# A hybrid decoder step on one core: another memory order of the weight slots, gating by the recurrence's groups, the first slice projected whole, token tiles padded to 128

## The chip, the cores and the metric

The kernel runs on one core of one Trainium2 chip, as one program that is launched once. The metric is the time of that core in microseconds (us) of the device; lower is better. A kernel's time is the median of several runs, and one further run is recorded by the hardware profiler. The engines are named as in the profile: PE is TensorE's matrix multiplication, PEld its loading of weights, DVE is VectorE, ACT is ScalarE, POOL is GpSimd and SP is SyncE, which here only issues DMAs.

## What is computed

The reference is one inference step of a two-layer decoder. 1104 rows of 1024 features go through it: 64 rows of eight decode requests, 16 learned rows and a prompt of 1024 tokens. Layer 0 is an mLSTM mixer, a recurrence over chunks of tokens; layer 1 is an attention with forget gates over one shared K and V. A SwiGLU feed-forward network (FFN) of width 2816 follows each. Cut to the part that the change touches, the mixer of layer 0 is:

```python
p = xn @ w_in                       # q, k, v, output gate og, gates gi and gf
li = softcap(gi + b_ig)
lf = log_sigmoid(softcap(gf + b_fg))
h, state = mlstm_sequence(q, k, v, li, lf, (C0, n0, m0), lead)
h = rmsnorm(h, mh_g)                # per head
out = (h.reshape(B, T, HV) * sigmoid(og)) @ w_out
```

After it come `x = x + out` and the FFN `x + (silu(xn @ w_gate) * (xn @ w_up)) @ w_down`, and then layer 1 in the same manner.

## The kernel before, in words

**Precision by three products.** Every large product is made of three matmuls (`mm3`, lines 270 to 273): operands are split into a rounded high half and a remainder, and high·high, high·low and low·high are added up. ACT makes the high half of a piece of weights (a cast, L333), DVE the low half (a subtraction, L334). A piece of 128 columns of a 1024-row weight is 512 KB.

**Tiling.** Rows are divided in two ways. The recurrence goes by nine chunks `TTA`, the first of 80 rows and eight of 128; its groups of three, `GRP`, span the ranges `TSA`: (0, 336), (336, 720), (720, 1104), at most `SLA` = 384 wide. Everything from the output projection on goes by three equal slices `TS` of `SL` = 368 rows, and where rows must lie on partitions, by tiles `TT` of 128, 128 and 112 rows in each slice. The split activations of slice t are in two tiles of `KT * SLA` columns (`flat_x`, made by `new_x`), of which a view `X[t]` shows only the rows that count.

**Gates of the recurrence.** `cache_prep` (L932) prepares the decode cache's forget values in a pool `cp` that is closed again, and stores them with eight DMAs on POOL's queue (L960). `rec_prep` (L965) then allocates the gate bias `gbias` and the initial `m0` in the pool `rp` and loads them over POOL's queue (L971 to L974). L1015 adds the bias to the gates, L1016 to L1019 and `log_sigmoid` turn them into `li` and `lf`, and TensorE transposes both (L1031).

**Recurrence.** In `recurrence` the orders of PE, DVE, ACT and POOL are fixed by the order in which the program names the instructions. Into the steps of the chunks a generator `rest_out` puts matmuls of the remaining q, k and og projections (`f(n)`: n steps of eight). When a group of chunks is done, `norm_heads` makes the factors of the per-head norm and scales the chunk's values (L1450). `gate_head` then takes one head of a group: TensorE transposes the values of its chunks (L1478), DVE multiplies them with the norm's gain and with the sigmoid of the output gate, which is loaded from DRAM (`ogD`) into a tile `og` or `ogc` (L1479), and `split` writes high and low halves into `X`. Two groupings exist for this: `GRPA`, chunks (0, 1, 2, 3), (4, 5, 6), (7, 8), for the norm, and `GG`, overlapping groups of chunks with row ranges that end at the ends of the slices, for the gating. From chunk 6 on, `g` calls `gate(0)` and then `gate(1)` in place of `f` once the projections are used up; what is left of group 1, and all of group 2, is gated in `mlp`.

**Output projection.** `mlp` (L479) allocates ten slots on the right side of the memory, 0 to 9 in that order; slots 0 and 1 are raw buffers for weights, 2 to 5 and 6 to 9 high and low halves. Layer 1 and its attention later take the same block: `both` (slots 0 and 1 in one), 7, 3, 8, 2. Pieces of `w_out` are loaded by SP (L537), m = 0, 3, 6 into a buffer of their own and the others into slots 0 and 1, and split. After the split of m = 1 the scaling of the last group's values (`late`) is put in DVE's order. `unit(t, m, x)` projects 128 output columns m of slice t (`fm_cols`, 24 matmuls), adds the result to the residual `H[t]`, and updates the sum of squares for the norm. PE's order is fixed there. With the mLSTM layer in front (`heads` given), three units of slice 0 stand first with the remaining heads of group 1 between them, and then units of slices 0 and 1 in turn, one head of group 2 after each; `mix.zero`, the work on slice 0 with which the FFN begins, starts after unit (0, 7). Layer 1 uses the `else` branch: slice 0 whole, then slice 1 with `mix.zero` between its units.

**Token tiles.** `tm_proj` and `first_values` use tiles of tokens as TensorE's stationary operand: `x_tile` returns columns a to b of `X[t]`, so that it is 128, 128 and 112 wide in a slice. `norm_x` fills `X` with the normed rows.

**Attention.** `last_gate` (in `attend_prompt`) and the projections before it read weights split into pairs of slots: the last one, m = 6, uses slots 3 and 8. `load_k` (L2551) loads the first pair of heads' q and k into the slots 2, 7, 3, 8 of layer 1 over SP's queue; `scores` (L2635) multiplies them.

Of the kernel before, what the change touches and what calls it, by code (L numbers as in the profile page):

```python
# [7 lines left out]
F32 = mybir.dt.float32  # L8
# [8 lines left out]
P = 128  # L17
# [17 lines left out]
GRPA = [(0, 1, 2, 3), (4, 5, 6), (7, 8)]  # L35
GG = [((0, 1, 2, 3), 0, TTA[3][1]), ((4, 5, 6), TTA[3][1], TS[1][1]), ((6, 7, 8), TS[2][0], T)]
# [218 lines left out]
class Net:  # L255
# [155 lines left out]
    def norm_x(self, H, t, g, sp, pp, inplace=False, psum=False):  # L411
# [68 lines left out]
    def mlp(self, H, w, l, heads=None, cb=None, early=None):  # L480
# [8 lines left out]
        with self.pool(self.uid("nsp")) as sp, self.pool(self.uid("npp"), bufs=2, space=PSUM) as pn:  # L489
# [16 lines left out]
            if cb:  # L506
                cw = cb
                wp = cw.enter_context(self.pool(self.uid("slots"), side="right"))
                slots = {x: wp.tile([P, self.wmin if x in (0, 1, 2, 3, *LOW[:2]) else KT * P], F32 if x < 2 else F32R,
                                    name=self.uid("slot")) for x in range(10)}  # L510
            else:
                cw, slots, ws = early
                wp = cw.enter_context(self.pool(self.uid("slots"), side="right"))
                for x in (4, 9, 5, 6):
                    slots[x] = wp.tile([P, KT * P], F32R, name=self.uid("slot"))
            with ExitStack() as c:
# [3 lines left out]
                if heads:  # L520
                    gp.tile([P, 4 * SL], F32, name="rest")
# [44 lines left out]
                if heads:  # L566
                    gate, *_ = heads(c.enter_context(self.pool("ghp", bufs=2, space=PSUM)), "gh",
                                     lambda n: gp.tile([P, SL], F32, name=n, tag="og", bufs=3), 1)
                    for x in range(3):
                        unit(0, x, x)  # L570
                        for _ in range(2):
                            gate(1)
                    while gate(1):
                        pass
                    load(nc.gpsimd, 1)
                    H2 = [2]
                    for t, m in ((0, 3), (1, 0), (1, 1), (0, 4), (1, 2), (0, 5), (1, 3), (0, 6), (1, 4), (0, 7), (1, 5),
                                 (1, 6), (1, 7)):
# [11 lines left out]
                else:  # L590
                    for m in range(KT):
                        unit(0, m, m)
                    run = mix.zero()
                    weights.load(0)
                    for m in range(KT):
                        unit(1, m, m)
                        next(run, None)
                        if m > 4:
                            next(run, None)
                    for _ in run:  # L600
                        pass
# [173 lines left out]
def phase_a(self, vt):  # L775
# [7 lines left out]
    with ExitStack() as c3:  # L783
# [105 lines left out]
        self.normed = set()  # L889

        def heads(pp, tag, op, deep):
# [3 lines left out]
            def ahead():  # L895
                while todo and len(ready) < 1 + deep:
                    t, h = todo.pop(0)
                    og = op(self.uid("ogc"))
                    _, a, b = GG[t]
# [10 lines left out]
            def gate(t):  # L910
                if not left[t] or t not in self.normed:
                    return False
# [17 lines left out]
        self.recurrence(kp, self.rec, v, qkD, rest, lambda gp: heads(pp, "mmA", lambda n: gp.tile([P, GG[0][2]], F32, name=n, tag="og", bufs=4), 2))  # L930
# [33 lines left out]
def rec_prep(self, kp, gates, rp, pp):  # L964
# [3 lines left out]
    if True:  # L968

        bias = rp.tile([P, 16], F32, name="gbias")  # L970
        nc.gpsimd.dma_start(bias[:, :8], I["b_ig_a"][0].partition_broadcast(P))  # L971
        nc.gpsimd.dma_start(bias[:, 8:], I["b_fg_a"][0].partition_broadcast(P))
        m0 = rp.tile([HA, NB], F32, name="m0")
# [111 lines left out]
def recurrence(self, kp, rec, v, qkD, fill, gate):  # L1085
# [18 lines left out]
    with ExitStack() as cr, self.pool("recAp", bufs=2, space=PSUM) as pp, \  # L1104
# [24 lines left out]
        with self.pool("rec2") as sets[2], self.pool("rec1", bufs=2) as rp, self.pool("rec3") as sets[0], \  # L1129
# [9 lines left out]
            for i in range(1, NT):  # L1139
# [21 lines left out]
                last = [g for g, z in enumerate(GRPA) if z[-1] == i]  # L1161
# [5 lines left out]
                if last:  # L1167
                    norm = self.norm_heads(last[0], v, rp)
# [5 lines left out]
                R, N = N, N2  # L1174
            rest()
# [252 lines left out]
def norm_heads(self, t, v, rp):  # L1428
# [3 lines left out]
    c = GRPA[t]  # L1432
    n = len(c)
    g = slice(c[0], c[-1] + 1)
    rd = rp.tile([P, len(GRPA[0]), HA], F32, name=f"rd{t}", tag="rd", bufs=1)[:, :n]
    f = self.fA[:, :n] if t == 2 else rp.tile([P, len(GRPA[0]), HA], F32, name=f"fA{t}", tag="fA", bufs=1)[:, :n]
# [16 lines left out]
    parts = [lambda x=x, i=i: part(x, i) for x, i in enumerate(c)]  # L1453
    if t == 2:
        self.late = parts
        self.normed.add(t)
        yield
        return
    for p in parts:
        p()  # L1460
        if p is parts[-1]:
            self.normed.add(t)
        yield
# [3 lines left out]
def gate_head(self, t, h, v, og, pp, tag):  # L1467

    nc = self.nc
    chunks, g0, g1 = GG[t]  # L1470
    if h == 0:
        for x in ((0, 1), (), (2,))[t]:
            self.new_x(x)
    o = TTA[chunks[0]][0]
    ps = pp.tile([P, 512], F32, name=self.uid("ghps"), tag=tag)
    for i in chunks:
        t0, t1 = TTA[i]
        nc.tensor.transpose(ps[:, t0 - o : t1 - o], v(i)[: t1 - t0, h, :DV], self.ident[: t1 - t0, : t1 - t0])  # L1478
    nc.vector.scalar_tensor_tensor(out=og, in0=ps[:, g0 - o : g1 - o], scalar=self.gain[:, G_MH + h : G_MH + h + 1],  # L1479
# [464 lines left out]
def first_values(self, fp, pp, norm):  # L1944
# [4 lines left out]
    for t in range(3):  # L1949
        vs = self.ny(f"vf{t}")[:, : 3 * 256].rearrange("p (i d) -> p i d", i=3)  # L1950
        for x, i in enumerate(GRP[t]):
            m = TT[i][1] - TT[i][0]
            ps = pp.tile([P, 512], F32, name=self.uid("tmps"), tag="f", bufs=2)
            for k in range(KT):
                wh, wl = halves[k // 4]
                xh, xl = self.x_tile(i, k)
                self.mm3(ps[:m, :256], xh, xl, wh[:, k % 4, :], wl[:, k % 4, :], k == 0, k == KT - 1)
# [915 lines left out]
```

## Time and profile before

| what | value |
|---|---|
| runs (3) | 2869.46, 2876.91, 2881.54 us |
| median | 2876.91 us |
| profiled execution | 2876.0 us |
| its span | 2874.3 us |
| mean granted clock | 0.991 |
| HBM traffic | 299.78 MB read, 96.77 MB written |

The span is what the profiler saw from the first to the last instruction; the rest of the execution's time lies around it. The page of the profile gives for each engine the time in which it was busy and its share of the span. A row of the timeline has the start, the duration, the engine, the line of the kernel, the operation with its output and inputs, their shapes and the number of such instructions in a row; a bracket behind it says how long the engine had been idle before and what released it. A row of the waits says which engine waited at which line for which work of which engine: the total in us, how many times, and the longest. A row of windows gives the busy time of PE, PEld, DVE, ACT and POOL in a stretch of the span, then the granted clock of TensorE (1 is full speed), the share of DMA time and GB/s.

### The profile page before, as it was taken

To read this page: it belongs to the slowest core of one execution; us is meant where nothing else is said; L and a number is where in the kernel's file an instruction comes from. 1 tells how busy PE (TensorE), PEld (TensorE's weight loads), DVE (VectorE), ACT (ScalarE), POOL (GpSimd) and SP (SyncE) were. 2 spreads that over 40 slices of the span, in tenths; PEclk is the share of its full clock that TensorE was granted. 3 is DMA by queue.
4 is the path that set the end of the run, shared out by engine and by line. 5 is a ranking of instruction groups with operands and counts; after the bars stand their busy time and mean duration, and the time that the engine had idled before them with its cause. 6 is when DMAs were issued, how large, how long until landed. Compare 5 with 4: busy or idle time off the path is not lost. (4 is left out here: it accounts for less than half of the span.)

```text
span 2874.3 us, 54148 instructions
## 1 busy us (share of the span) xinstructions
PE 2786.1 (97%) x20638; PEld 2662.6 (93%) x20638; DVE 1742.2 (61%) x3598; ACT 1317.1 (46%) x2629; POOL 1074.1 (37%) x1578
## 2 busy tenths in 40 slices
PE   8898998999999999999999998999999999999999
PEld 7887988999999999999999887777899999999998
DVE  6034564787877755553365542677468778775553
ACT  6122464444444434443344553777444444443432
POOL 3022333156666411117563201455316566641110
PEclk9999999999999999999999999999999999999999
DMA  6136655222222275544453685443412222237653
GB/s 216 38 101 164 172 166 158 76 75 84 84 78 78 81 276 202 194 151 149 135 168 115 221 302 184 166 146 119 152 52 83 80 84 83 79 98 246 211 194 107
DMA packets 314070, 400.08 MB, mean 139 GB/s; under 512 B 28998, under 2 KB 235826, under 8 KB 312786
## 3 DMA queue, kind: packets, MB, share of 16 engines
q1 hardware_dynamic: 277282, 277.66, 30.4%
q0 software_dynamic: 35776, 118.40, 12.4%
q8 instruction: 162, 2.65, 0.4%
q14 instruction: 98, 0.80, 0.1%
q10 hardware_dynamic: 752, 0.57, 0.1%
HBM read 299.78 MB, written 96.77 MB: 138 GB/s over the span
## 5 line engine op out<-in xcount | busy, mean ns | idle before, releaser
L334 DVE TENSOR_TENSOR slot<-slot,slot 128x1024 fp32r<-128x1024 f32 (+3 forms) x263 | 250.7, 955 | 115.9 <-ACT slot L333 111.5
L333 ACT CAST slot<-slot 128x1024 fp32r<-128x1024 f32 (+3 forms) x263 | 206.5, 787 | 229.1 <-PE dps L272 98.6
L1541 PE MATMUL m<-x0h,slot 128*128 128x368 f32 x640 | 178.5, 330 | 0.0
L1541 PE MATMUL m<-x1h,slot 128*128 128x368 f32 x640 | 174.0, 331 | 2.7 <-DVE ns L1518 0.9
L1647 POOL DMA_DIRECT2D hr<-hT x60 | 32.5, 542 | 280.2 <-DVE T_2l L334 68.5
L1541 PE MATMUL m<-x2h,slot 128*128 128x368 f32 x480 | 132.5, 330 | 0.0
L113 POOL TENSOR_TENSOR slot<-vA 128x256 f32<-128x256 f32 x80 | 75.6, 955 | 151.9 <-DMA vA<-in_w_gate_up 78.0
L113 POOL TENSOR_TENSOR slot<-Ht 128x256 f32<-128x256 f32 x80 | 75.1, 949 | 150.8 <-DMA Ht<-in_w_gate_up 79.2
L334 DVE TENSOR_TENSOR slot<-Ht,slot 128x256 fp32r<-128x256 f32 (+3 forms) x101 | 88.7, 880 | 55.7 <-ACT slot L333 55.7
L334 DVE TENSOR_TENSOR slot<-vA,slot 128x256 fp32r<-128x256 f32 (+3 forms) x101 | 88.4, 877 | 55.8 <-ACT slot L333 55.8
L409 POOL TENSOR_TENSOR ns<-ns,nq 128x368 f32<-128x368 f32 x50 | 54.1, 1083 | 178.8 <-ACT nq L407 178.1
L1541 PEld LDWEIGHTS m<-x1h,slot 128*128 128x128 f32 x640 | 115.6, 188 | 4.6 <-DVE vA L1517 1.4
L1541 PEld LDWEIGHTS m<-x0h,slot 128*128 128x128 f32 x640 | 116.1, 188 | 0.0
L1541 PE MATMUL m<-x1l,slot 128*128 128x368 f32 x320 | 105.5, 330 | 0.0
L1541 PE MATMUL m<-x0l,slot 128*128 128x368 f32 x320 | 105.5, 330 | 0.0
L2667 ACT ACTIVATE s<-s,nb 128x272 f32<-128x272 f32 (+7 forms) x126 | 98.8, 786 | 0.6 <-POOL nb L2658 0.6
L2702 ACT COPY th<-tp 128x768 f32<-128x768 f32 (+1 forms) x80 | 73.5, 920 | 47.7 <-PE tp L2694 27.4
L1541 PE MATMUL m<-T_2h,slot 128*128 128x368 f32 x320 | 94.0, 334 | 0.0
L1541 PE MATMUL m<-T_4h,slot 128*128 128x368 f32 x320 | 93.5, 333 | 0.0
L328 DVE SCALAR_TENSOR_TENSOR slot<-slot,gain,slot 128x256 fp32r<-128x256 f32 (+2 forms) x152 | 63.8, 468 | 44.6 <-ACT slot L327 42.2
L334 DVE TENSOR_TENSOR slot<-wr,slot 128x1024 fp32r<-128x1024 f32 x42 | 53.5, 1274 | 59.1 <-ACT slot L333 59.1
L1541 PEld LDWEIGHTS m<-x2h,slot 128*128 128x128 f32 x480 | 86.9, 188 | 0.0
(861 smaller groups left out, 10360.7 us busy)
## 6 DMA issues: line engine op xcount, KB each, us to landing
slot<-in_w_down SPq DMA_DIRECT2D x88, 512.0 KB, 4.3
hr<-hT POOLq DMA_DIRECT2D x60, 368.0 KB, 5.6
wr<-in_w_down SPq DMA_DIRECT2D x42, 512.0 KB, 4.1
wraw<-in_w_in_a SPq DMA_DIRECT2D x40, 512.0 KB, 4.2
vA<-in_w_gate_up SPq DMA_DIRECT2D x40, 512.0 KB, 4.0
Ht<-in_w_gate_up SPq DMA_DIRECT2D x40, 512.0 KB, 4.0
kp<-in_cache_k SPq DMA_DIRECT2D x32, 512.0 KB, 6.9
vp<-in_cache_v SPq DMA_DIRECT2D x32, 512.0 KB, 9.6
```

Of the source, the lines that this page charges most:

```text
L113: self.net.nc.gpsimd.tensor_tensor(out=o, in0=a, in1=b, op=op)
L328: nc.vector.scalar_tensor_tensor(out=lo[:, k], in0=raw[:, k], scalar=gk, in1=hi[:, k].bitcast(F32), op0=ALU.mult, op1=ALU.subtract)
L333: self.nc.scalar.copy(hi, src)
L334: self.nc.vector.tensor_tensor(out=lo, in0=src, in1=hi.bitcast(F32), op=ALU.subtract)
L409: (nc.vector if x >= late else nc.gpsimd).tensor_tensor(out=s, in0=s, in1=sq, op=ALU.add)
L1541: nc.tensor.matmul(u.b[b][:, :SL], w[p][:, k], x[q][:, k], start=new and k == i == 0, stop=k == 1 and i == 2, skip_group_check=True)
L1647: nc.gpsimd.dma_start(hraw[j], hT[t][:, 2 * c : 2 * c + 2])
L2667: nc.scalar.activation(ss[z, u], ss[z, u], AF.Exp, bias=nb[:, z : z + 1], accum_out=sm[:, u, z : z + 1])
L2702: nc.scalar.copy(th.rearrange("p x z (u h q) -> p h (x z u) q", h=2, q=64)[:, :, :n], pt[:, :, :n])
```

## The change

Five things change.

1. `gbias` and `m0` are allocated in `kp` and no longer in `rp`.
2. The ten slots are allocated in the order 3, 8, 0, 1, 2, 7, 5, 6, 4, 9.
3. `GRPA` and `GG` go. The norm of heads and the gating both go by `GRP` and `TSA`: after the chunks 2, 5 and 8, three chunks each. A head's rows of a group now belong to one slice or two, and `part` splits them into the slices they belong to. One more `gate(1)` stands after the last chunk, so that groups 0 and 1 are gated within the recurrence, and the tiles `og` are `SLA` wide.
4. In `mlp` slice 0 is projected whole, with 0, 1, 2, 1, 2, 1, 1, 0 heads of group 2 after its eight units; slice 1 follows, with `mix.zero` between its units, in both layers.
5. `x_tile` returns 128 columns of `flat_x`, except where `tm_proj` is asked for a single tile (`only`); `norm_x` clears the columns behind the slice's 368 with a memset on POOL for each of the two halves, so that the third tile's other 16 columns are zero.

```diff
-GRPA = [(0, 1, 2, 3), (4, 5, 6), (7, 8)]
-GG = [((0, 1, 2, 3), 0, TTA[3][1]), ((4, 5, 6), TTA[3][1], TS[1][1]), ((6, 7, 8), TS[2][0], T)]
...
-    def x_tile(self, i, k):
+    def x_tile(self, i, k, m=P):
...
-        t = i // 3
-        o = ts[t][0]
-        a, b = tt[i][0] - o, tt[i][1] - o
-        xh, xl = self.X[t]
-        return xh[:, k, a:b], xl[:, k, a:b]
+        a = k * SLA + tt[i][0] - ts[i // 3][0]
+        return [x[:, a : a + m] for x in self.flat_x[i // 3]]
...
             m = t1 - t0
+            w = m if only is not None else P
...
-                xh, xl = self.x_tile(i, k)
-                self.mm3(ps[:m, :n], xh, xl, wh[:, k % 4, :], wl[:, k % 4, :], k == 0, k == KT - 1)
+                xh, xl = self.x_tile(i, k, w)
+                self.mm3(ps[:w, :n], xh, xl, wh[:, k % 4, :], wl[:, k % 4, :], k == 0, k == KT - 1)
...
         xh, xl = self.new_x(t)
+        for x in self.flat_x[t]:
+            nc.gpsimd.memset(x.rearrange("p (k n) -> p k n", k=KT)[:, :, n:].bitcast(F32), 0.0)
...
-                                    name=self.uid("slot")) for x in range(10)}
+                                    name=self.uid("slot")) for x in (3, 8, 0, 1, 2, 7, 5, 6, 4, 9)}
...
                 if heads:
                     gate, *_ = heads(c.enter_context(self.pool("ghp", bufs=2, space=PSUM)), "gh",
-                                     lambda n: gp.tile([P, SL], F32, name=n, tag="og", bufs=3), 1)
-                    for x in range(3):
-                        unit(0, x, x)
-                        for _ in range(2):
-                            gate(1)
-                    while gate(1):
-                        pass
+                                     lambda n: gp.tile([P, SLA], F32, name=n, tag="og", bufs=3), 1)
                     load(nc.gpsimd, 1)
-                    H2 = [2]
-                    for t, m in ((0, 3), (1, 0), (1, 1), (0, 4), (1, 2), (0, 5), (1, 3), (0, 6), (1, 4), (0, 7), (1, 5),
-                                 (1, 6), (1, 7)):
-                        unit(t, m, m)
-                        if not gate(2) and H2:
-                            load(nc.gpsimd, H2.pop())
-                        if (t, m) == (0, 7):
-                            run = mix.zero()
-                            weights.load(0)
-                        elif t and m > 4:
-                            for _ in range(3):
-                                next(run, None)
...
+                for m in range(KT):
+                    unit(0, m, m)
+                    for _ in range((0, 1, 2, 1, 2, 1, 1, 0)[m] if heads else 0):
+                        gate(2)
+                    if heads and m == KT - 2:
+                        load(nc.gpsimd, 2)
+                run = mix.zero()
+                weights.load(0)
+                for m in range(KT):
+                    unit(1, m, m)
+                    next(run, None)
+                    if m > 4:
                         next(run, None)
-                    for _ in run:
-                        pass
+                for _ in run:
+                    pass
...
-        bias = rp.tile([P, 16], F32, name="gbias")
+        bias = kp.tile([P, 16], F32, name="gbias")
...
-        m0 = rp.tile([HA, NB], F32, name="m0")
+        m0 = kp.tile([HA, NB], F32, name="m0")
...
-                if last:
-                    norm = self.norm_heads(last[0], v, rp)
+                if i % 3 == 2:
+                    norm = self.norm_heads(i // 3, v, rp)
...
                 R, N = N, N2
+            gate(1)
             rest()
...
-    chunks, g0, g1 = GG[t]
+    g0, g1 = TSA[t]
...
-    for i in chunks:
+    for i in GRP[t]:
         t0, t1 = TTA[i]
-        nc.tensor.transpose(ps[:, t0 - o : t1 - o], v(i)[: t1 - t0, h, :DV], self.ident[: t1 - t0, : t1 - t0])
+        nc.tensor.transpose(ps[:, t0 - g0 : t1 - g0], v(i)[: t1 - t0, h, :DV], self.ident[: t1 - t0, : t1 - t0])
```

More of the change, by code (lines that the diff above doesn't have):

```diff
@@ L520, in mlp @@
                 if heads:
-                    gp.tile([P, 4 * SL], F32, name="rest")
+                    gp.tile([P, 4 * SL - 128], F32, name="rest")
                 wp = c.enter_context(self.pool(self.uid("wo")))
@@ L567, in mlp @@
                     gate, *_ = heads(c.enter_context(self.pool("ghp", bufs=2, space=PSUM)), "gh",
-                                     lambda n: gp.tile([P, SL], F32, name=n, tag="og", bufs=3), 1)
-                    for x in range(3):
-                        unit(0, x, x)
-                        for _ in range(2):
-                            gate(1)
-                    while gate(1):
-                        pass
-                    load(nc.gpsimd, 1)
-                    H2 = [2]
-                    for t, m in ((0, 3), (1, 0), (1, 1), (0, 4), (1, 2), (0, 5), (1, 3), (0, 6), (1, 4), (0, 7), (1, 5),
-                                 (1, 6), (1, 7)):
-                        unit(t, m, m)
-                        if not gate(2) and H2:
-                            load(nc.gpsimd, H2.pop())
-                        if (t, m) == (0, 7):
-                            run = mix.zero()
-                            weights.load(0)
-                        elif t and m > 4:
-                            for _ in range(3):
-                                next(run, None)
-                    for _ in run:
-                        pass
[L590 to L596, printed above, removed]
+                                     lambda n: gp.tile([P, SLA], F32, name=n, tag="og", bufs=3), 1)
+                    load(nc.gpsimd, 1)
+                for m in range(KT):
[10 more added lines that the diff above has]
+                    if m > 4:
                         next(run, None)
[L598 to L601, printed above, removed]
+                for _ in run:
+                    pass
                 run = mix.one()
@@ L888, in phase_a @@
         left = {t: list(range(HA)) for t in range(3)}
-        self.normed = set()
         def heads(pp, tag, op, deep):
@@ L910, in gate @@
             def gate(t):
-                if not left[t] or t not in self.normed:
+                if not left[t]:
                     return False
@@ L929, in phase_a @@
         next(rest)
-        self.recurrence(kp, self.rec, v, qkD, rest, lambda gp: heads(pp, "mmA", lambda n: gp.tile([P, GG[0][2]], F32, name=n, tag="og", bufs=4), 2))
+        self.recurrence(kp, self.rec, v, qkD, rest, lambda gp: heads(pp, "mmA", lambda n: gp.tile([P, SLA], F32, name=n, tag="og", bufs=4), 2))
     return heads
@@ L1160, in recurrence @@
                 squares = self.chunk_out(i, R, rp, *args, den, ssq, g, exp=N2 and N2["exp"])
-                last = [g for g, z in enumerate(GRPA) if z[-1] == i]
-                if last:
+                if i % 3 == 2:
                     for _ in squares:
@@ L1166, in recurrence @@
                 next(norm, None)
-                if last:
-                    norm = self.norm_heads(last[0], v, rp)
+                if i % 3 == 2:
+                    norm = self.norm_heads(i // 3, v, rp)
                 if i == 5:
@@ L1431, in norm_heads @@
     tm, den, ssq = self.fin
[L1432 to L1436, printed above, removed]
+    g = slice(3 * t, 3 * t + 3)
+    rd = rp.tile([P, 3, HA], F32, name=f"rd{t}", tag="rd", bufs=1)
+    f = self.fA if t == 2 else rp.tile([P, 3, HA], F32, name=f"fA{t}", tag="fA", bufs=1)
     nc.vector.scalar_tensor_tensor(out=rd, in0=den[:, g], scalar=-1.0, in1=den[:, g], op0=ALU.mult, op1=ALU.max)
@@ L1452, in part @@
             op=ALU.mult)
-    parts = [lambda x=x, i=i: part(x, i) for x, i in enumerate(c)]
+    parts = [lambda x=x, i=i: part(x, i) for x, i in enumerate(GRP[t])]
     if t == 2:
         self.late = parts
-        self.normed.add(t)
         yield
@@ L1460, in norm_heads @@
         p()
-        if p is parts[-1]:
-            self.normed.add(t)
         yield
@@ L1469, in gate_head @@
     nc = self.nc
-    chunks, g0, g1 = GG[t]
+    g0, g1 = TSA[t]
     if h == 0:
-        for x in ((0, 1), (), (2,))[t]:
-            self.new_x(x)
-    o = TTA[chunks[0]][0]
+        self.new_x(t)
     ps = pp.tile([P, 512], F32, name=self.uid("ghps"), tag=tag)
-    for i in chunks:
+    for i in GRP[t]:
         t0, t1 = TTA[i]
-        nc.tensor.transpose(ps[:, t0 - o : t1 - o], v(i)[: t1 - t0, h, :DV], self.ident[: t1 - t0, : t1 - t0])
-    nc.vector.scalar_tensor_tensor(out=og, in0=ps[:, g0 - o : g1 - o], scalar=self.gain[:, G_MH + h : G_MH + h + 1],
+        nc.tensor.transpose(ps[:, t0 - g0 : t1 - g0], v(i)[: t1 - t0, h, :DV], self.ident[: t1 - t0, : t1 - t0])
+    nc.vector.scalar_tensor_tensor(out=og, in0=ps[:, : g1 - g0], scalar=self.gain[:, G_MH + h : G_MH + h + 1],
                                    in1=og, op0=ALU.mult, op1=ALU.mult)
```

4 lines of the change are left out of this document (2 added, 2 removed).

## The prediction

> **What bounds the kernel now.** I read the page first: one engine is busy almost all the time.
>
> ```profile
> span 2874.3 us, 54148 instructions
> PE 2786.1 (97%) x20638; PEld 2662.6 (93%) x20638; DVE 1742.2 (61%) x3598; ACT 1317.1 (46%) x2629; POOL 1074.1 (37%) x1578
> ```
>
> TensorE is the bound, and 2874.3 − 2786.1 = 88.2 us of the span is all that waits can give back; beyond that only matmuls that run faster count. So the question for every part of the change is which TensorE gap it touches. The gaps were then looked up by place: the gate bias (136 to 149 us), the end of the recurrence and the start of the output projection (420 to 478), the FFN's start (553 to 640), the start of the prompt's attention (1782 to 1791). The profiled execution took 2876.0 us against a median of 2876.91 in three runs; I sum against 2876.0 and add 0.9. A measurement of this kernel can tell about 0.5% (14 us) from no change.
>
> **Gate bias and m0 in `kp` instead of `rp`.**
>
> ```profile
> 135.58 0.60 PE L954 MATMUL csps<-ident,lp 128*128 128x128 f32 x4
> 149.26 2.04 PE L1031 MATMUL rps<-ident,gates 80*8 80x80 f32 x9 [13.09 <-DVE gates L1017]
> 148.26 0.31 DVE L1015 TENSOR_TENSOR gates<-gates,gbias 128x144 f32<-128x144 f32 x1 [6.68 <-DMA gbias<-in_b_fg_a]
> 139.34 4.25 POOL L960 DMA_DIRECT2D csE<-cs  x8 [1.46 <-DVE clast L958]
> 144.12 0.55 POOL L972 DMA_DIRECT2D gbias<-in_b_fg_a  x1
> 4.74 0.22 POOL L991 MEMSET cap<- 128x128 f32 x1
> ```
>
> Columns: start, duration, engine, line, operation, and in brackets the idle time before it with its releaser. The bias is loaded into memory that cache_prep had used, so its DMAs are issued behind the eight stores of csE, at 144, and land at 148; the gate addition waits for that, and TensorE idles 13.09 us. `cap`, allocated from `kp` in the same function, is filled at 4.74 us: nothing had used its memory. In `kp` the bias can be loaded as early. Then what is late next? DVE is free after its cumulative sum:
>
> ```profile
> 139.40 0.98 DVE L1035 MEMSET rs<- 8x1104 f32 x1 [0.17 <-issue]
> 159.36 0.78 PE L1031 MATMUL rps<-ident,lf_tm 80*8 80x80 f32 x6
> 155.57 0.23 DVE L352 SCALAR_TENSOR_TENSOR lf_tm<-lf_tm,lsw 128x72 f32<-128x72 f32 x1
> ```
>
> The addition can stand where rs is cleared now, at 139.2 or before, and TensorE's nine transposes of the input gates have their operand before TensorE asks. The log-sigmoid behind it takes 155.80 − 148.26 = 7.5 us from addition to end; 139.2 + 7.5 = 146.7. TensorE transposes that result at 159.36 in before; without the gap it asks for it at 159.36 − 13.09 = 146.3. So 0.4 us of new wait, and 1.4 if the 0.98 us memset goes first. Taken: −12.7; ends −11.7 and −13.1.
>
> **The recurrence's tail.** Gating by the recurrence's own groups removes the wait of gate transposes for the scaled values, 2.4 us, but scales a group of three chunks at a time, close to the end, where each chunk costs half of the second row:
>
> ```profile
> PE ghps L1478 <- DVE vA L1450: 2.4, 2, 1.7
> 456.26 2.35 DVE L1450 TENSOR_TENSOR vA<-vA,fA 128x1024 f32<-128x1024 f32 x2
> ```
>
> The extra `gate(1)` and the changed counts move about one such 1.18 us scaling ahead of work that TensorE waits for. Transposes per head go from 4+3+3 to 3+3+3, splits from 2+1+1 to 1+2+2: one small instruction each way. Taken −1.0; ends −2.4 and +1.2.
>
> **The junction into the output projection.** Order of the slots decides where w_out's raw pieces m = 1 and 2 land. In before slots 0 and 1 lie first, over the buffers of the recurrence's gates; their load is issued only at 441.60. In after, slots 3 and 8 lie there and slots 0 and 1 over the old weight buffers, which are last read by the split of 429.13.
>
> ```profile
> PE pops L271 <- ACT wo L333: 5.5, 2, 4.0
> PE pops L273 <- DVE wo L334: 1.3, 2, 0.7
> 441.60 0.99 SPq L537 DMA_DIRECT2D slot<-in_w_out_a  x2
> 429.13 1.22 DVE L319 TENSOR_TENSOR wlo<-wraw,whi 128x1024 fp32r<-128x1024 f32 x1
> DMA to landing us min/median/max: 4.3/4.7/9.5
> 445.31 1.23 DVE L334 TENSOR_TENSOR wo<-woraw,wo 128x1024 fp32r<-128x1024 f32 x1 [1.90 <-ACT wo L333]
> 452.43 1.28 ACT L902 ACT_TABLE_LOAD   x1 [7.16 <-DMA ogc<-ogD]
> 450.00:460.00 10.00, 5.38 (x24) 4.81 (x23) 4.88 (x5) 5.18 (x7) 0.53 (x2) 0.79 0.36 101
> 460.00:470.00 10.00, 9.78 (x53) 9.36 (x52) 9.45 (x13) 6.08 (x9) 4.32 (x6) 0.87 0.97 287
> ```
>
> The first two rows are waits (total, times, longest) from 443 to 478; the two last give per stretch the busy time of PE, PEld, DVE, ACT and POOL, then the granted clock. Both longest waits, 4.0 and 0.7, belong to m = 1. It would land by 430.4 + 4.7 = 435 instead of 446 and could be cast straight behind m = 0. But one thing more held it: ACT sits 7.16 us before the table load at 452.43, waiting for a gate input, and the cast of m = 1 stands behind that sigmoid in its order. In after the first slice's units come first, with no gate after unit 0, so the cast should stand ahead of the sigmoid; then the low half of m = 1 is done by about 449.5, and TensorE asks for it near 450.4. The wait for m = 0 (1.5 + 0.6) stays. Gone: 4.0 + 0.7 = 4.7. The clock: (1 − 0.79) × 5.38 + (1 − 0.87) × 9.78 = 2.4 us of slow matmuls behind that gap. Taken −7.1; ends −3 (half of it) and −9 (with the small waits that the two rows leave out).
>
> Is the first slice's pace kept? A unit is 24 matmuls: at 53 in 9.78 us it takes 4.4 us, so eight take about 35. DVE has in it 8 low halves at 1.23, three scalings at 1.18, and for 8 accumulations, 8 gate products and 16 split pieces, 0.25 to 0.6 each, some 15: 28 us in all. It fits, with little to spare.
>
> **The FFN's start.** The loop now is layer 1's own: `mix.zero` runs between slice 1's units and not after them.
>
> ```profile
> PE m L1541 <- DVE vA L1517: 3.0, 2, 2.1
> PE m L1541 <- ACT vA L1547: 1.7, 2, 1.1
> PE m L1541 <- DVE Ht L1517: 2.2, 2, 1.4
> PE m L1541 <- DVE ns L1518: 0.9, 1, 0.9
> PE m L1541 <- ACT Ht L1547: 0.6, 1, 0.6
> 620.00:630.00 10.00, 10.00 (x53) 10.00 (x53) 7.82 (x11) 3.16 (x7) 7.54 (x8) 0.85 0.17 50
> ```
>
> The first two waits are layer 0's, the next three layer 1's, where that order runs already: 4.7 against 3.7 us. And the 10 us after layer 0's waits ran at a clock of 0.85, which costs 1.5. Taken −1.0 − 1.5 = −2.5; ends 0 and −6.2 (every wait and the clock). The Trainium skill, "TensorE: Matmul & The Clock Gate", Part 1, says that the clock falls after an idle window of about 3.4 us; the trace has 0.85 behind gaps of 2.1 us at most, so it does not follow that rule here. By the rule the 1.5 us has another cause and stays, and the sum would be 1.5 us more.
>
> **Token tiles padded to 128.** The third tile of each slice has 112 columns in TensorE's stationary operand and gets 128, in 864 matmuls. The trace has both widths side by side, 24 matmuls of 112 and then 48 of 128:
>
> ```profile
> 1299.74 0.28 PE L271 MATMUL tmps<-slot,x1h 128*112 128x256 f32 x1
> 1302.62 0.28 PE L271 MATMUL tmps<-slot,x2h 128*128 128x256 f32 x1
> 1308.27 0.28 PE L271 MATMUL tmps<-slot,x2h 128*112 128x256 f32 x1
> L273 PEld LDWEIGHTS tmps<-slot,x1l 128*112 128x112 f32 x96 | 17.1, 178 | 0.0
> L272 PEld LDWEIGHTS tmps<-slot,x1h 128*128 128x128 f32 x192 | 36.1, 188 | 0.0
> ```
>
> (1302.62 − 1299.74) / 24 = 120.0 ns a matmul at 112 and (1308.27 − 1302.62) / 48 = 117.7 at 128, although the load itself reads 178 and 188 ns. Nine groups of 96 are 864 matmuls: 864 × (117.7 − 120.0) = −2.0 us; ends 0 and −4. The 80-wide first tile of the projections ahead of the recurrence is padded too: taken as nothing, by the same rows. The six pad memsets are on POOL, 0.22 us or less each by the row of `cap`, 37% busy: nothing. If they delayed a norm it would be 1.3 us. The Trainium skill, same page, section "LDWEIGHTS (loading the stationary operand)", has the load grow with the columns, so padding should cost; the two load rows agree in sign, the pitch does not.
>
> **The attention's start.** `both` and slots 7, 3, 8, 2 of the second layer take the upper end of the same block, so the new order also changes what they lie over.
>
> ```profile
> PE sp L2635 <- DMA slot<-qDl: 4.5, 1, 4.5
> 1784.32 0.34 PE L2635 MATMUL sp<-slot,slot 64*128 64x144 f32 x2 [2.29 <-DMA slot<-kDh]
> PE sp L2635 <- DMA slot<-kDl: 1.6, 1, 1.6
> SPq L2551 <- PE bps L273: 15.3, 1, 15.3
> 1779.06 0.34 SPq L2551 DMA_DIRECT2D slot<-qDh  x1
> 1759.70 0.33 PE L271 MATMUL bps<-x0h,slot 128*128 128x368 f32 x1
> ```
>
> SyncE holds the loads of the first pair's q and k for 15.3 us, until the gate projection's last weights (pair 3 and 8) are read, at 1779. In after slots 3 and 8 lie lowest, outside the new tiles, and the last one that overlaps belongs to m = 5, whose last matmul is at 1759.70. The loads can leave 1779.06 − 15.3 = 1763.8 or a little after, and TensorE, which wants them from 1784.32 − 2.29 = 1782.0 on, finds them there: it had the first of them 5.3 us after its issue at 1779.06 and the last 12 us after, and would now have 18. Taken −4.5 − 2.3 − 1.6 = −8.4; ends −4 (the scores behind are paced by DVE, which might only move the gap) and −8.4.
>
> **Sum.** 12.7 + 1.0 + 7.1 + 2.5 + 2.0 + 8.4 = 33.7: 2876.0 − 33.7 = 2842.3, with 0.9 for the median 2843.2; forecast 2843. Best ends: 13.1 + 2.4 + 9 + 6.2 + 4 + 8.4 = 43.1, so 2834. Worst: 11.7 − 1.2 + 3 + 0 + 0 + 4 = 17.5, so 2859.
>
> **Rivals.**
> - *The junction's gain is lost* (0.13): m = 1 lands early, but its cast still stands behind a sigmoid that waits for ogc, as the 7.16 us row shows. All 7.1 stay: 2850.
> - *The attention's 8.4 come back later* (0.11), because DVE, at one row of maxima per score tile, sets the pace from the first tile on. Against it: TensorE's waits there are for DMA. 2851.
> - *The bias stays behind csE* (0.08): POOL issues in order, and if the loads are put where the code has them, they go out at 144 whatever the memory. This is the case in which that part doesn't do what it says. 2843 + 13 = 2856.
> - *Wider weight loads set the pace* (0.05): if the 10 ns between the two load rows counted in full, 864 × 10 = 8.6 us more instead of 2.0 less: 2854. [...]
> - *Slower: weights arrive too late for the first slice* (0.03). Projecting slice 0 whole needs a new weight pair every unit from the start, where before five units of slice 1 stood between. One piece takes 4.7 to 9.5 to land, 1.05 and 1.23 to split: 7 to 12 us, and three raw buffers give it three units, 13 us. It decides once that chain is over 13 us; then pieces 2 to 7 each cost what m = 1 does now, 4.7 + 2.4: 6 × 7.1 = 43, and 2850 + 43 = 2893. For it speaks the 0.97 DMA share at 460; against it, the medians.
>
> **How the numbers follow.** The forecast has 0.60. The four next cases lie at 2850 to 2856, inside the worst end. The range runs from 2832 (best end, less 2 for the spread of a median) to 2860; outside are the slower rival and combinations of two losses. Faster by over 0.5% is below 2862.5: forecast and the four cases, 0.97, less 0.08 for two or more of them together: 0.89. Within 0.5%: 0.07. Slower: 0.04.
>
> **What would show it.** The DMAs of gbias near 5 us and no gap before L1031; w_out pieces issued at 424 to 431 and TensorE's wait for ACT there at 1.5 to 2; no DMA wait at L2635, SyncE's wait at L2551 gone; tile pitch near 118 ns everywhere; TensorE's idle time down from 88 to about 57 us. A new wait at pops for weights of m = 2 to 7, or DVE at its limit from 450 to 485, would prove me wrong.

## The result, and the profile after

| kernel | runs | median | ratio to before |
|---|---|---|---|
| before | 4 | 2875.69 us | |
| changed | 4 | 2846.61 us (2842.61 to 2847.67) | 0.9897, 95% interval 0.9873 to 0.992 |

The change saves about 29 us, 1.0%; the forecast's sum was 33.7. The profiled execution took 2846.91 us with a span of 2845.2, at a granted clock of 0.994. From the page:

```profile
span 2845.2 us, 54159 instructions
PE 2778.5 (98%) x20630; PEld 2657.1 (93%) x20630; DVE 1748.0 (61%) x3606; ACT 1317.9 (46%) x2637; POOL 1083.5 (38%) x1584
```

Idle time of TensorE fell from 88.2 to 66.7 us, busy time by 7.6. So about a quarter of the gain is not waits at all but matmuls that run faster, and the forecast of 57 us idle was not met. Where the time went is read by following the same instruction in both traces; what it starts or ends earlier by is the changed kernel's lead:

| place | before, us | changed, us | lead |
|---|---|---|---|
| transposes of the forget gates end | 161.67 | 149.54 | 12.1 |
| last key sums of the recurrence end (`kps`) | 408.78 | 397.33 | 11.5 |
| output projection starts (`pops`) | 445.33 | 438.86 | 6.5 |
| slices 0 and 1 projected, `mp` starts | 558.71 | 549.62 | 9.1 |
| FFN's down projection starts (`dps`) | 1017.20 | 1006.83 | 10.4 |
| last token tile ends (`tmps`) | 1607.74 | 1592.44 | 15.3 |
| gate projection of layer 1 ends (`bps`) | 1779.03 | 1763.01 | 16.0 |
| first transposed probabilities (`tp`) | 1810.45 | 1782.92 | 27.5 |
| last scores (`sp`) | 2019.42 | 1990.08 | 29.3 |

Three places gave nearly all of it, and one that was to give 8.1 (the recurrence's end and the junction) lost 2.4 in this pair of executions. Each kernel stands here with one execution. Two more profiled executions of the changed program (the runs act_first and changed_again below) show how far such a number can be trusted: from the forget gates to the last key sums the three took 247.8, 244.7 and 242.1 us.

**Gate bias.** TensorE's timeline after the change:

```profile
135.82 0.60 PE L934 MATMUL csps<-ident,lp 128*128 128x128 f32 x4
137.82 0.78 PE L1011 MATMUL rps<-ident,gates 80*8 80x80 f32 x6 [1.40 <-ACT csl L935]
148.08 0.78 PE L1011 MATMUL rps<-ident,lf_tm 80*8 80x80 f32 x6 [0.95 <-ACT whi L331]
```

The gap of 13.09 is 1.40, and a new one of 0.95 stands before the transposes of the log-sigmoid, within the 0.4 to 1.4 us that the forecast allowed.

**The junction.** Waits of TensorE from 430 to 490 and from 400 to 443, then ACT's, SyncE's and POOL's timelines:

```profile
PE pops L269 <- ACT wo L331: 5.1, 2, 3.2
PE pops L271 <- DVE wo L332: 0.9, 2, 0.7
```

```profile
PE mmA L269 <- ACT stg L841: 2.3, 1, 2.3
PE ghps L1451 <- ACT stg L841: 0.9, 1, 0.9
```

```profile
410.61 0.52 ACT L882 ACTIVATE ogc<-ogc 128x384 f32<-128x384 f32 x1 [2.76 <-DMA ogc<-ogD]
412.68 0.50 ACT L841 COPY stg<-mmA 128x384 f32<-128x384 f32 x1
446.06 1.28 ACT L882 ACT_TABLE_LOAD   x1 [7.25 <-DMA ogc<-ogD]
447.78 1.98 ACT L331 CAST wo<-slot 128x1024 fp32r<-128x1024 f32 x2
409.59 13.49 SPq L535 DMA_DIRECT2D slot<-in_w_out_a  x2
442.37 1.61 POOL L881 DMA_DIRECT2D ogc<-ogD  x3 [3.45 <-DMA ogD<-stg]
```

The raw pieces m = 1 and 2 do go out early, at 409.59 and 422.71 by SyncE's rows, ahead of the forecast's 424 to 431. But the cast of m = 1 still stands at 447.78, behind the table load and the sigmoid, which wait 7.25 us for the output gate. The wait of 4.0 became 3.2, not nothing. And ahead of it TensorE now waits for copies of `stg` that stand in ACT's order behind sigmoids of heads whose gates have not landed: the row at 410.61 and the one behind it. Older waits went in exchange: from the last key sums to `mp` TensorE's busy time leaves 11.1 us of idle time before and 11.4 after. What makes this stretch 2.4 us longer is the clock, whose mean over it was 0.98 before and 0.96 after.

**FFN's start.** The waits here are 2.7 and 0.6 us, in place of 3.0 and 1.7:

```profile
PE m L1514 <- DVE vA L1490: 2.7, 2, 1.8
PE m L1514 <- ACT vA L1520: 0.6, 1, 0.6
600.00:610.00 10.00, 7.66 (x40) 7.04 (x39) 10.00 (x12) 5.11 (x10) 9.92 (x10) 0.91 0.40 123
610.00:620.00 10.00, 9.88 (x55) 9.57 (x53) 7.80 (x12) 3.37 (x8) 7.53 (x7) 0.92 0.07 22
```

The slow clock stays, in two windows in place of one: (1 − 0.91) × 7.66 + (1 − 0.92) × 9.88 = 1.5 us, as much as the forecast had counted as gone. Windows of 1 us show what such a mean consists of:

```profile
608.00:609.00 1.00, 0.95 (x4) 0.95 (x5) 1.00 (x2) 0.50 (x1) 1.00 (x2) 0.62 0.19 54
609.00:610.00 1.00, 1.00 (x5) 1.00 (x5) 1.00 (x1) 0.00 (x0) 1.00 (x2) 0.50 0.96 270
610.00:611.00 1.00, 1.00 (x5) 1.00 (x4) 1.00 (x2) 0.00 (x0) 1.00 (x1) 0.50 0.67 200
611.00:612.00 1.00, 1.00 (x6) 1.00 (x5) 1.00 (x2) 0.00 (x0) 1.00 (x3) 0.67 0.00 0
```

The clock is at half for (0.38 + 0.50 + 0.50 + 0.33) / 0.5 = 3.4 us and full around it. Whether such a stretch follows the wait differs between executions. The first two rows are of another execution of the same program (act_first, longest wait 1.6 us). The two behind them are a wait and a window of the kernel with the padding alone, which has the order of before:

```profile
600.00:610.00 10.00, 7.86 (x45) 7.25 (x45) 10.00 (x12) 4.65 (x9) 9.92 (x10) 1.00 0.46 143
610.00:620.00 10.00, 8.18 (x48) 7.58 (x47) 8.18 (x14) 4.43 (x10) 8.61 (x9) 1.00 0.01 2
```

```profile
PE m L1541 <- DVE vA L1517: 3.0, 2, 2.1
620.00:630.00 10.00, 9.06 (x54) 8.76 (x53) 8.17 (x11) 3.16 (x7) 7.89 (x8) 1.00 0.18 52
```

The wait of 2.1 us is that of before, and no slow clock follows it. A slow stretch stands at the FFN's start in 2 of the 5 profiled executions with the order of before and in 2 of the 9 with the changed one, and it costs nothing that can be seen: from `mp` to the down projection the first two took 458.5 and 459.0 us and the other three 458.3, 458.9 and 459.0. In those without it TensorE waits 0.9 us more for DVE, so what it wins there is waited for.

**Attention's start.** SyncE issues the first of the loads 18 us and the last 16 us ahead of the first score, which waits for nothing. The windows (PE, PEld, DVE, ACT, POOL, clock) stand first for before and then for the changed kernel, from the end of the gate projection on:

```profile
1747.70 0.42 SPq L2524 DMA_DIRECT2D slot<-qDh  x1
1765.94 0.56 PE L2608 MATMUL sp<-slot,slot 64*128 64x144 f32 x6
```

```profile
1779.00:1811.00 32.00, 23.62 (x140) 18.41 (x139) 11.24 (x57) 11.83 (x22) 10.15 (x23) 0.84 0.84 294
1811.00:1900.00 89.00, 84.04 (x1167) 62.78 (x1167) 62.97 (x313) 69.93 (x144) 45.32 (x121) 0.98 0.42 141
```

```profile
1763.00:1783.00 20.00, 20.00 (x129) 15.71 (x129) 11.27 (x57) 11.26 (x21) 10.10 (x23) 1.00 0.84 277
1783.00:1872.00 89.00, 84.18 (x1198) 63.49 (x1200) 64.23 (x320) 71.83 (x150) 45.37 (x122) 1.00 0.42 142
```

Besides 8.4 us of waits, (1 − 0.84) × 23.62 + (1 − 0.98) × 84.04 = 5.5 us of slow clock are gone: 13.9 by these rows, 13.3 by the leads. The gap that DVE was said to pass on is not there. The slow clock behind these longer waits comes every time: in all five profiled kernels with the old order of slots its mean over these 32 us is 0.79 to 0.84.

### The profile page after: what moved, and what is told of

The parts are those of the page before. It is cut to its first block, busy times and chain, and to the rows that moved or that the text cites. A ratio compares the mean times of both kernels' runs of the same rounds, so it can differ in the third digit from the quotient of the medians.

```text
span 2845.2 us, 54159 instructions
## 1 busy us (share of the span) xinstructions
PE 2778.5 (98%) x20630; PEld 2657.1 (93%) x20630; DVE 1748.0 (61%) x3606; ACT 1317.9 (46%) x2637; POOL 1083.5 (38%) x1584
```

## The experiments

Twelve runs followed, each in five rounds; each is compared with before on the same chip (2874 to 2875 us). Four take parts of the change alone, and one is the changed kernel once more.

**Bias alone** (`gbias` only; `m0` stays in `rp`):

```diff
-        bias = rp.tile([P, 16], F32, name="gbias")
+        bias = kp.tile([P, 16], F32, name="gbias")
```

> Before, with gbias alone allocated in kp; m0 stays in rp. Theory 1 (the two traces): the 13.1 us gap goes, 0.9 to 1.5 us of new waits for the log-sigmoid come, and TensorE is 10.5 to 12.4 us ahead from there to the end: 2863.3 to 2865.2 against 2875.7. Rival (the forecast's full term): 12.7, so 2863.0, with nothing given back in the preparation that follows. Rival 2: m0, still issued behind the eight stores of csE, takes the bias's place as what is late: gain under 5 us, 2871 or more.

Measured: 2866.59 us, ratio 0.9975 (0.9964 to 0.9986), 8.1 less by the medians; the profiled execution is 9.9 us shorter than before's. Its lead is 12.2 at the forget gates, and 11.5 at the end of the last projection. Theory 1 holds at the place; the median is 1.4 us above its range. In the profiled execution 2.8 us are given back by `mp`, where the clock was 0.96 against 0.97 in before. m0 does not take the bias's place.

**Slots alone** (the order of ten slots, nothing else):

> Before, with the ten slots in the order 3, 8, 0, 1, 2, 7, 5, 6, 4, 9. Theory 1: the raw piece m = 1 lands early but its cast stays behind the sigmoid that waits for the output gate, so the waits of 5.5 and 1.3 us at the junction stay within 1 us of what they were; at the attention's start 8.4 us of waits go and 4 to 5.5 us of slow clock behind them: in all -12.5 to -14, 2862 to 2863. Rival (the forecast): junction -7.1 and attention -8.4, in all -15.5, 2860, with ACT's wait at the junction down to 1.5. The time can hardly tell these apart; the waits at the junction do.

Measured: 2863.55, ratio 0.9963 (0.9949 to 0.9976), 11.1 less. ACT's waits and TensorE's at the junction, then windows and waits at the attention's start:

```profile
PE pops L271 <- ACT wo L333: 4.1, 2, 2.6
ACT L902 <- DMA ogc<-ogD: 5.8, 1, 5.8
1775.00:1796.00 21.00, 21.00 (x149) 16.59 (x149) 11.23 (x57) 12.14 (x23) 10.18 (x23) 1.00 0.85 271
```

The wait for ACT went from 5.5 to 4.1 us and its longest from 4.0 to 2.6, so most of the expected 4.0 did not come. The lead grows by 1.5 at the junction and by 13.2 from the gate projection to the last score. That is theory 1 for the attention's start, and nearly so for the junction: the waits for ACT fell by 1.4 us where it allowed 1.

**Padding alone:**

> Before, with the token tiles padded to 128 and nothing else. Theory 1: matmuls follow each other in 113 ns with 128 columns and in 120 with 112, so 864 of them give 5 to 6 us back, of which the two traces show 4.8: 2870 to 2871. Rival (the forecast): 117.7 against 120.0 ns, -2.0, 2873.7. Rival 2: the wider loads cost 10 ns each, +8.6, 2884.

Measured: 2869.09, ratio 0.9974 (0.9966 to 0.9983), 5.6 less. That is theory 1. Rows of before from later groups of the same work show why: 39 matmuls lie between the first two, 9 between the last two.

```profile
1464.37 0.28 PE L273 MATMUL tmps<-slot,x2l 128*128 128x256 f32 x1
1468.79 0.28 PE L273 MATMUL tmps<-slot,x2l 128*128 128x256 f32 x1
1468.90 0.28 PE L271 MATMUL tmps<-slot,x2h 128*112 128x256 f32 x1
1469.98 0.28 PE L271 MATMUL tmps<-slot,x2h 128*112 128x256 f32 x1
```

4.42 / 39 = 113.3 ns at 128 columns, 1.08 / 9 = 120.0 at 112: 6.7 ns × 864 = 5.8 us. The 117.7 of the forecast isn't an error of reading: matmuls of 128 columns have two paces, and each holds for whole groups. The first two rows are of the changed kernel's execution, 72 matmuls apart, and the last two of act_first, the same program, 27 apart:

```profile
1283.65 0.28 PE L269 MATMUL tmps<-slot,x1h 128*128 128x256 f32 x1
1292.13 0.28 PE L269 MATMUL tmps<-slot,x2h 128*128 128x256 f32 x1
1283.45 0.28 PE L269 MATMUL tmps<-slot,x1h 128*128 128x256 f32 x1
1286.51 0.28 PE L269 MATMUL tmps<-slot,x1h 128*128 128x256 f32 x1
```

8.48 / 72 = 117.8 ns and 3.06 / 27 = 113.3. Counted over stretches of more than six, 412 of these matmuls go in before at the slower pace and 1142 at the faster; in the changed kernel it is 549 and 1773, in act_first 5 and 2313. What sets the pace is open.

**Groups and first slice left out** (before with `gbias` in kp, the new slots and the padding):

> The changed kernel without the gating by the recurrence's groups and without the first slice projected whole: before, plus gbias in kp, the new order of the slots, and the padding. Theory 1: groups and first slice together cost 2.4 us between the last chunks and the end of the projection and give 1.3 at the FFN's start, so this kernel is at 2844 to 2847, no slower than the changed one at 2846.6. Rival (the forecast): they gave 3.5 us, and the junction's gain needs the first slice's order, 7.1: this kernel then is 3 to 10 us slower than the changed one, 2850 to 2857.

Measured: 2848.92, ratio 0.9905 (0.9891 to 0.992). The changed kernel's ratio in three sets is 0.9885 to 0.9897. By the medians groups and first slice are worth 2 to 6 us beside the other parts, but the intervals overlap, so that nothing isn't ruled out. Theory 1 (no slower than the changed one) leans the wrong way, and neither is settled by this run.

**The casts put first.** The three casts are put under the order of the program:

```diff
-first.enter_context(self.tc.manual_schedule(engines={E.PE, E.SP, *([E.DVE] if heads else [])}))
+first.enter_context(self.tc.manual_schedule(engines={E.PE, E.SP, *([E.DVE, E.Activation] if heads else [])}))
```

> The changed kernel, with ACT's order in the stretch of the first three w_out pieces held to the program's, so that the casts of m = 0, 1 and 2 stand ahead of the sigmoid that waits for the output gate. Theory 1 (the cast, not the landing, held unit (0, 1)): the waits of 3.2 and 0.3 us before unit (0, 1) go, and with them 2.6 us of slow clock; the wait of 1.8 and 0.7 for m = 0 stays: -5 to -6.5, 2840 to 2842. Rival (the forecast's other half: the landing sets it): waits as they were, 2846.6. Rival 2: the sigmoid, now later, holds the first gate of group 2, and the wait moves to DVE's gate product: 2845 to 2847.

Measured: 2843.05, ratio 0.9885 (0.987 to 0.99). This is a miss of the experiment: the edit fixes the casts among themselves, the sigmoid isn't under it, and every engine's instructions stand in the order that they had in the changed kernel. The waits are the same (3.2 us). So it tells only how well a time and a trace repeat: 2846.6 and 2843.05 are the same program. A third execution of it (changed_again) has 5.0 us in place of the 3.2 before unit (0, 1).

**The same with the old slots,** and so the changed kernel with the slots 0 to 9:

> The kernel of the run before (the changed kernel with the casts ahead of the sigmoid), with the slots in the old order 0 to 9 again. Theory 1: raw piece m = 1 then waits for the last gate, near 435, lands near 440 and is split by 442.5, ahead of unit (0, 1) at 444.5: nothing is lost at the junction, only the attention's start loses 13 us: 2853 to 2855. Rival (the order of the slots is what the junction needs): a wait of 3 to 4 us and its clock come back as well: 2858 to 2861.

Measured: 2857.8, ratio 0.9934 (0.9921 to 0.9948): 14.8 more than with the new order. The rival is nearer: besides the attention's start, 4.0 us of lead are lost between the start of the projection and `mp`. In waits of TensorE, and ACT's and POOL's timeline:

```profile
PE pops L269 <- ACT wo L331: 8.7, 2, 7.2
446.06 1.28 ACT L882 ACT_TABLE_LOAD   x1 [9.65 <-DMA ogc<-ogD]
441.73 1.61 POOL L881 DMA_DIRECT2D ogc<-ogD  x3 [5.42 <-DMA ogD<-stg]
```

It isn't the landing of m = 1 that does it: its cast is still behind the sigmoid. But two 512 KB pieces now go out at 433.0 and 437.8, around the last stores of the output gates (435.07); POOL waits 5.42 us for these in place of 3.45, and ACT 9.65 in place of 7.25. The kernels with the order of before agree: POOL waits 3.8 us there with the old slots and 1.9 with the new. That the pieces hold the stores up is argued from these times.

**Late sigmoids,** one head ahead no longer:

```diff
-                for x in ready[: deep]:
+                for x in ready[: 1]:
```

> The changed kernel, with the sigmoid of an output gate put into ACT's order only when its own head is gated, in the recurrence too, and no longer a head ahead. Theory 1 (the loss of some 4.5 us between 409 and 432 comes from sigmoids that wait for their load ahead of copies that TensorE needs): the waits for the copies of stg, 2.3 and 0.9 us, go and of the rest half: -2.5 to -4.5, 2842 to 2844. Rival: the gate product now waits for the sigmoid and holds TensorE's next transposes and projections: 2846 to 2850.

Measured: 2843.55, ratio 0.9886 (0.9871 to 0.9902): not told apart from the changed kernel. In the trace the wait for the copy of stg falls from 2.3 to 1.2 us or less and 2.7 us are won by the start of the output projection, 1.4 of them by the last key sums; waits for DVE's gate product rise (4.2 for 1.9 us in sum), and the wait before unit (0, 1) is 4.6. From the last key sums to the start of the output projection it took 40.2 us, where three executions of the changed kernel took 41.0 to 42.7. Whether the wait behind it takes this back is not shown: it was 3.2, 3.2 and 5.0 in those three, and 2.5 in the next run.

**Both orders:**

> The changed kernel with both changes of ACT's order: casts of the first three w_out pieces ahead of the sigmoid, and each sigmoid only when its head is gated. Theory 1: the two stretches follow each other, so the gains add up: 2837 to 2840. Rival: one of the two only moves its wait, so no better than the better one of them, 2840 to 2844.

Measured: 2843.89, ratio 0.9887 (0.9872 to 0.9902). Since the first of the two edits moves nothing, it is the run before once more, and says nothing on adding up. Here the wait before unit (0, 1) is 2.5 us.

**Gate tiles elsewhere.** The load of the first gates in the output projection waits for the stores of `stg`, because its tiles lie over `stg`. The spacer below them, which the change also made 128 columns narrower, is cut in two:

```diff
-                    gp.tile([P, 4 * SL - 128], F32, name="rest")
+                    gp.tile([P, 208], F32, name="rest")
...
+                if heads:
+                    gp.tile([P, 4 * SL - 128 - 208], F32, name="rest1")
                 run = mix.zero()
```

> The changed kernel, with the three tiles for the output gates of group 2 lower in memory, over state tiles that are done with by 421 us, and no longer over the buffers stg from which the last output gates are stored; the spacer that was below them is split around them, and nothing else moves. Theory 1 (the cast of m = 1 stands behind a sigmoid whose load waits until those stores have read stg): the loads go out 3.4 us earlier, the sigmoid runs near 442.6 instead of 446.1, unit (0, 1) finds its weights within 0.5 us, and 1 to 2.5 us of slow clock go with the wait of 3.2: -3.5 to -6 against the changed kernel (2843 to 2847 so far): 2838 to 2842. Rival (the load takes that long wherever its tile lies): waits as they were, 2843 to 2847.

Measured: 2844.26, ratio 0.9897 (0.9882 to 0.9911). POOL's and ACT's timelines and the waits of TensorE:

```profile
434.66 1.73 POOL L883 DMA_DIRECT2D ogc<-ogD  x3
439.13 1.28 ACT L884 ACT_TABLE_LOAD   x1 [4.57 <-DMA ogc<-ogD]
PE pops L269 <- ACT wo L331: 2.4, 2, 1.9
PE ghps L1453 <- DVE ogc L1454: 3.7, 3, 2.8
```

The mechanism is shown: POOL's loads wait for nothing, ACT waits 4.57 in place of 7.25, and of the 3.2 us before unit (0, 1) 0.6 is left. The time does not follow: a wait of 2.8 us for a gate product comes some 17 us later, in place of 1.0, and from the start of the projection to `mp` only 1.2 us are won. Its profiled execution is within the spread of the changed kernel's three.

**Both:**

> The kernel of the run before, and each sigmoid in the recurrence only when its own head is gated. Theory 1: the late sigmoids gave 2.7 us by the end of the last projection, and lost them to a longer wait (4.6 for 3.2 us) at unit (0, 1), because what releases it follows the last store; with that wait gone they are kept: 2 to 3 us less than the run before, 2836 to 2839. Rival: some other wait takes them again, as at the first gates of group 2: the same as the run before within 1 us.

Measured: 2841.31, ratio 0.9884 (0.9869 to 0.9899). From the start of the projection to `mp` 2.6 us are won, and the lead at its end is 7.8, part of which arose before 250 us, where no edit lies. From the last key sums to `mp` it took 148.5 us, against 151.9 to 153.0 in three executions of the changed kernel, so the waits that were aimed at are less. The median is 3.0 us below that of the run before, as theory 1 had it, but the intervals overlap, and those of the changed kernel's sets (0.9885 to 0.9897) do too: no version is shown to beat it.

**Groups and first slice alone,** beside **the changed kernel again:**

> Before, with the gating by the recurrence's groups and the first slice projected whole, and nothing else: the bias in rp, the slots in the old order, 112 columns in the third tile. Theory 1 (the traces: 5 us lost in ACT's order from 409 to 432, 1.3 won at the FFN's start, and with the old order of the slots 4 us more lost before unit (0, 1), where the run with the old slots waited 7.2 us): 3 to 8 us slower than before, 2877 to 2882. Rival (the forecast's split: 1.0 at the recurrence's end, 2.5 at the FFN's start, the junction's 7.1 from the slots): 3.5 us faster, 2871. Rival 2: slots and order work apart from each other: +1, 2875.

> The changed kernel itself, beside the run before on the same chip. If the parts simply add up, it is faster than the run before by what bias, slots and padding gave alone (8.1 + 11.1 + 5.6 = 24.8 us by the medians): with 2880 there, 2855, which its first runs (2846.6) already speak against. Theory 1: the order of the slots is worth 4 us more here than alone, so 29 us or more lie between the two: 2844 to 2848.

Measured: 2874.71, ratio 1.0003 (0.9994 to 1.0012), and 2841.7, ratio 0.9892 (0.9877 to 0.9908). Alone, the two parts do nothing that can be measured; 33.0 us lie between the two kernels, where the sum of bias, slots and padding alone gives 24.8. From the waits of TensorE and ACT's timeline of the first:

```profile
PE pops L269 <- ACT wo L331: 7.0, 2, 5.5
456.19 1.28 ACT L882 ACT_TABLE_LOAD   x1 [9.55 <-DMA ogc<-ogD]
```

In its profiled execution this kernel, with the old order of slots, loses 6.3 us from the last key sums to `mp` and wins 2.0 at the FFN's start. It was not 3 to 8 slower, as theory 1 had it; the profiled execution is 1.8 longer than before's. The time from the last key sums to `mp`, in us, one number for each profiled execution of a kernel whose output gates lie and are ordered as in before or in the changed kernel (bias and padding lie outside this stretch), separates the two parts:

| slots | order of before | by groups, first slice whole |
|---|---|---|
| old | 149.9, 151.4, 152.7 | 155.8, 156.2 |
| new | 148.3, 148.4 | 151.9, 152.3, 153.0 |

The new slots save 3.0 us there without the groups and 3.6 with them, by the means; groups and first slice cost 4.0 to 4.7. At the FFN's start (`mp` to the down projection) they win: 456.4 to 457.4 us in nine executions against 458.3 to 459.0 in five. That the order of the slots is worth more with the groups than without, as 33.0 against 24.8 and 14.8 against 11.1 us suggest, is not clear of the intervals, and the junction does not show it.

## Why the prediction was right, and where it wasn't

The time was right and its split was not: two terms were too small by about 8 us together and hid one that failed by 10. That these cancelled is luck.

- **Gate bias,** −12.7: right. 12.1 us at the place, also with this part alone. By the end of the recurrence 11.5 are left.
- **Recurrence's end and junction,** −1.0 and −7.1: failed; together they cost 2.4 in the pair of traces, and about 1 by the means of the table above, where the slots save 3.0 to 3.6 and the groups and the first slice cost more. Two steps broke. "In after the first slice's units come first, with no gate after unit 0, so the cast should stand ahead of the sigmoid" took ACT's order from the text of the program, but only PE, SyncE and DVE keep that there; ACT's order is the planner's, and it had the sigmoid first, as the rival with 0.13 said. And the sigmoid's wait was taken as given, though it begins at POOL's loads of ogc, which wait 3.45 us for the stores that still read the memory below their tile. Moving the tile removed POOL's wait for them, and ACT's fell from 7.25 to 4.57 us. For the recurrence's end the forecast looked at DVE's scalings; what came is ACT, whose sigmoids wait for loads ahead of copies that TensorE needs (2.3 and 0.9 us).
- **FFN's start,** −2.5: 1.3 measured. The two waits fell as in layer 1, from 4.7 to 3.3 us, but the 1.5 us of slow clock stayed in this execution. The forecast tied it to these waits and took it as time; in 10 of 14 profiled executions it isn't there, and the stretch is no shorter without it. By the rule that the forecast took from the Trainium skill, "TensorE: Matmul & The Clock Gate", Part 1, the term would have been 1.0. Its reason is not shown: the gap before the slow clock is 1.8 us here, short of the rule's 3.4, and a gap of 2.1 in the kernel with the padding alone is followed by none.
- **Padding,** −2.0: right in direction, too small: 4.9 us of lead, 5.6 by its own run. The 117.7 ns were read from a stretch at the slower of the two paces that 128 columns show; most of the work goes at 113.3. A "tile pitch near 118 ns everywhere" was not met. That the load of 128 columns reads 188 ns and not 178 costs nothing here, so the rival that priced it at 8.6 us is out. The Trainium skill, "TensorE: Matmul & The Clock Gate", section "LDWEIGHTS (loading the stationary operand)", has the load's time grow with the columns. It does in the records, by 10 ns; the distance of the matmuls behaves the other way.
- **Attention's start,** −8.4: 13.3 by the leads. The waits were right; the clock behind them was left out, although the same sum had been made for the junction. It measured 5.5 us by the windows.
- **Rivals.** The bias did not stay behind csE (issued at 4.7 us); DVE gave nothing back in the scores, where its waits are 7.8 us before and 7.6 after; w_out's pieces for m = 3 to 7 were not late.

Open: what groups and first slice are worth in all, since the junction and the FFN's start together show a loss of 2 to 3 us while the medians show none (alone) or a gain of 2 to 6 (beside the other parts). Stretches that no edit touches, as from 160 to 250 us, differ between executions of the same program in part by the clock: its mean there was 0.94, 0.96 and 0.98 in the three of the changed kernel.

## What to carry to other kernels

Read the order of an engine from the trace, or from what fixes it, before a wait is taken as removed: an earlier landing is worth nothing while the instruction that uses it stands behind another that waits. When a gap of TensorE goes, look for the slow clock behind it as well, at every gap by the same sum, and in more than one execution: behind the attention's waits it came five times of five, at the FFN's start four times of fourteen, and cost nothing there. A lead of a few us between two single traces is not yet an effect. And where a memory order is changed, ask for each tile whose last reader it must outlast; a store that still drains counts as one.

## What the runs showed of the hardware that was not expected

A matmul of 256 columns with 112 columns of weights follows its predecessor in 120.0 ns, one with 128 in 113.3 or 117.8, and the share of the two paces changes between executions of one program. The slow clock at the FFN's start is a stretch of 3.4 us at half speed that follows the waits there in 4 of 14 executions, the largest of them 2.1 us or less. After the gaps of 1.6 to 4.5 us at the attention's start the granted clock is 0.84 over 32 us; without them it is 1.00 over the same work, in all nine executions with the new slots. The same program, measured in three sets, gave 2846.6, 2843.05 and 2841.7 us.
